# A two-layer decoder trunk: fp32 diagonal blocks in the attention, three kept experts with a tile-pair tail, and a branch prefetch hint

## The chip, the cores and the metric

The kernel runs on one core of a Trainium2 chip. The metric is the device time of one execution in microseconds (us), the median of several runs; lower is better. The engines are TensorE (PE; its weight loads are shown as PEld), VectorE (DVE), ScalarE (ACT), GpSimd (POOL) and SyncE (SP).

## The reference

Two layers work on x, 512 tokens of width 1024 in float32. Each layer is a token mixer and then a mixture of experts, each followed by `x = layer_norm(alpha * x + f(x))`. The mixer of layer 0 is a chunked gated linear attention. That of layer 1 is a sparse attention with three branches (compressed, selected and window), each a causal softmax of the scores times values, mixed by gates. What the change touches, cut down:

```python
smask = (kpos <= qpos[:, None])                       # causal: the diagonal block is half masked
p_slc = masked_softmax(jnp.einsum('bghqd,bgqkd->bghqk', qb, k_sel), smask)
o_slc = jnp.einsum('bghqk,bgqkd->bghqd', p_slc, v_sel)
p_win = masked_softmax(jnp.einsum('bghqd,bgkd->bghqk', qb, kw_b), wmask)
o_win = jnp.einsum('bghqk,bgkd->bghqd', p_win, vw_b)
...
gate = jnp.zeros((n, 16)).at[arange(n)[:, None], top_e].set(w)     # two experts of 16 per token
h = silu(einsum('nd,edf->nef', xt, w_gate)) * einsum('nd,edf->nef', xt, w_up)
return einsum('nef,efd->nd', h * gate[:, :, None], w_down)         # D 1024, hidden 256
...
y = (x - mean) * rsqrt(var + 1e-5) * g + b                         # layer_norm over 1024
```

## The kernel before, in words

The 512 tokens are four tiles of 128 rows, t = 0 to 3. Nearly all products are made of three float16 products: both operands are split into a high and a low float16 part (hi and lo), and hi·hi, hi·lo and lo·hi are summed in a PSUM bank of 512 float32 columns. The splits of the weights (L179 on ACT, L181 on DVE) run beside the products on PE. In time the program is: the linear attention (0 to about 235 us), the experts of layer 0 (to about 412), the projections of the sparse attention and the attention itself (to about 768), the experts of layer 1 (to about 960) and the tail, the last normalisation and the stores.

**The experts** (`moe`). Each expert has 96 slots. For expert e a one-hot matrix of tokens by slots is made on POOL (L828, one instruction per tile), and PE collects the expert's rows with it (L839, 64 matmuls). Gate and up products are L910 to L912, the gate of each slot is summed on PE at L915, the down product is L944 to L946. Experts 0 to 13 write their weighted output to the DRAM buffer `yslots` (ACT copies at L953, a DMA issued by ACT at L955). When expert 13 has been issued, eight indirect DMAs on POOL's queue (L959) gather the rows of `yslots` and add them into x. The last `KEEP = 2` experts, 14 and 15, stay in SBUF as hi and lo (`yh`, L949 on ACT, L950 on DVE). Their one-hot matrices are transposed (L856, L857) to `ohT`, and `add_last` brings their outputs back to the tokens with one-hot products (L359, per tile and half 2 experts x 2 parts) and adds the bank to x: on DVE (L369), or by a copy on ACT (L366) and an add on POOL (L367).

**The fallback** (`dense_moe`). Behind expert 0's gate and up products stands a block for the case that an expert has more than 96 tokens. Every engine loads a number (L966) and compares it (L967); here the block is jumped over in both layers. It holds some 870 of PE's 23,700 instructions.

**The tail** (`finish_out`). All four tiles go through `add_last` (three halves on DVE, five on ACT and POOL). Then, for the pair (0, 1) and then (2, 3), come the statistics of the rows on DVE (L331, L311), the chain of small instructions that ends with the inverse deviation z (L312 to L317, one chain per tile), and the scaling: four halves by two DVE instructions (L344, L345), four by one on ACT (L347) and two on POOL (L348, L349). Each half is then stored (L1574, issued by SP).

**The attention** (`nsa_attn`). It goes over query tiles t = 3, 2, 1, 0, four groups g of four heads, and two branches b. `scores` computes for every key block j up to t the scores (L1418, L1419), the exponential to float32 `pf` (L1421 on ACT), on the diagonal block j = t a mask on POOL (L1424), and the split into `ph` hi and lo: hi on ACT (L1386, a second exponential from PSUM, or L1388, a copy) or DVE (L1390), lo on POOL (L1392) or DVE (L1394), by the turns in `HI_BY` and `LO_BY`. `pv` multiplies each block with V, three matmuls per head and block (L1435 to L1437). `combine` divides and adds (L1458 to L1468, DVE and POOL). `evac_v` writes V from PSUM (L1224 ACT, L1225 DVE). In between PE works on the output projection (L257 to L259).

The order on each engine is that of a scheduler that records the operations. Pools of buffers decide how early a step can start: `ph` lies in the three buffers of the weights' staging tag `wst`.

Of the kernel before, what the change touches and what calls it, by code (L numbers as in the profile page):

```python
# [21 lines left out]
NT = 4  # L22
# [9 lines left out]
PUMPS = (5, 5, 5, 5, 5, 5, 5, 5, 5, 5, 5, 5, 5, 8, 5, 4, 5, 5, 5, 5)  # L32
HI_BY = 'daeeee'
LO_BY = 'pdp'
OUT_ADD = (0, 0), (1, 0), (1, 1), (1, 1)
OUT_DVE = 1, 5, 6, 7
OUT_DIR = -1
# [15 lines left out]
NSU = 4  # L53
NHL = dict(l=4, a=3)
RINGS = "aaallll" * 3 + "aaalllll" * 3 + "aaa", "aaallll" * 7
KEEP = 2
HS = 16.0
NEG = -1e30


class Trunk:
# [258 lines left out]
    def finish_out(self, store):  # L320
        nc = self.nc
        V = nc.vector
        lng, lnb = self.moe_ln
        scales, after = {}, None
        for t in range(NT):
            self.add_last(t, OUT_ADD[t])
        for pair in ((0, 1), (2, 3)):
            for t in pair:
                for n in range(2):
                    with self.behind(after):  # L330
                        last = V.bn_stats(self.bns[t][:, n], self.x[t][:, n * 512:n * 512 + 512])  # L331
            for t in pair:
                with self.behind(last):
                    self.bn = self.bns[t]
                    _, mean, z, b = self.ln_scale()
                    after = V.scalar_tensor_tensor(b, mean, -1.0, z, op0=OP.mult, op1=OP.mult)
                scales[t] = mean, z, b
            for t in pair[::OUT_DIR]:
                mean, z, b = scales[t]
                for h in range(2):  # L340
                    hs = slice(h * 512, h * 512 + 512)
                    s, g, o = self.x[t][:, hs], lng[:, hs], lnb[:, hs]
                    if 2 * t + h in OUT_DVE:
                        V.scalar_tensor_tensor(s, s, mean, g, op0=OP.subtract, op1=OP.mult)  # L344
                        V.scalar_tensor_tensor(s, s, z, o, op0=OP.mult, op1=OP.add)  # L345
                    else:
                        nc.scalar.activation(s, s, AF.Identity, bias=b, scale=z)  # L347
                        nc.gpsimd.tensor_mul(s, s, g)  # L348
                        nc.gpsimd.tensor_add(s, s, o)  # L349
                    store(t, h)  # L350

    def add_last(self, t, pool=()):
        self.bns[t] = self.tmp([P, 2, 6], F32, "bn", 4)
# [456 lines left out]
    def moe(self, layer, xT, ahead=()):  # L810
# [153 lines left out]
    def dense_moe(self, layer, xT, gm, ci):  # L964
        nc, tc, a = self.nc, self.tc, self.a
        load = nc.values_load(ci[0:1, 0:1], min_val=0, max_val=2 * S)  # L966
        with tc.If(load > CAP, preferred_fallthrough_block=False):  # L967
            dm = self.tmp([P, NT, NE], F32, "rt_dm", 1)
            nc.vector.tensor_scalar(dm, gm, IWS / HS, None, op0=OP.mult)
            with tc.For_i(0, NE, 1) as e:  # L970
                buf = self.row("dw")
                st, hl = buf[:, :512], buf[:, 512:].bitcast(F16).rearrange("p (i n) -> p i n", i=2)

                def load_piece(i, c):
                    src = a["moe"][layer, bass.ds(e, 1), i].rearrange("o p f -> (o p) f")
# [12 lines left out]
                for i in range(2):  # L988
                    b = banks[2 * i:2 * i + 2]
                    for c in range(4):  # L990
                        w = load_piece(i, c)
                        for f in range(2):
                            for t in range(NT):
                                o = b[f][:, t * P:(t + 1) * P]
                                for k in range(2):
                                    s = slice(k * 256 + f * P, k * 256 + f * P + P)
                                    x = [xT[t][u][:, c * 2 + k] for u in range(2)]
                                    product(o, [v[:, s] for v in w], x, c == k == t == 0,
                                            (c, k, t) == (3, 1, NT - 1))
# [73 lines left out]
    def nsa_proj(self, first, PT):  # L1073
# [8 lines left out]
        kA = [PT([P, 4, S], f"kA{b}") for b in range(2)]  # L1082
        kB = [PT([P, 4, S], f"kB{b}") for b in range(2)]
        V = [[PT([P, 4, 129], f"V{b}{t}") for t in range(NT)] for b in range(2)]
        qA = [PT([P, NT, 4, P], f"qA{g}") for g in range(4)]
        qB = [PT([P, NT, S], f"qB{g}") for g in range(4)]
        gate = PT([P, NT, 16, 3], "gate", F32)
# [285 lines left out]
        return (kcA, kcB, vc, kA, kB, V, qA, qB, gate), rest  # L1373

    def nsa_attn(self, T, pool, early, rest, kcA, kcB, vc, kA, kB, V, qA, qB, gate):
# [5 lines left out]
        def split(hi, lo, src, ps=None):  # L1381
            i = cnt[0]
            cnt[0] += 1
            how = HI_BY[i % len(HI_BY)]
# [28 lines left out]
        def scores(t, g, b):  # L1413
            ph = self.wp.tile([P, 4, 2, S], F16, name="ph", tag="wst", bufs=NST)
            for j in range(t, -1, -1):
# [4 lines left out]
                pf = T([P, S], "pf", F32, 3)  # L1420
# [5 lines left out]
                split(ph[:, j, 0], ph[:, j, 1], pf, None if j == t else st)  # L1426
            return ph

        def pv(t, g, b, ph):
            ob = self.bank()  # L1430
            for h in range(4):
                hs = slice(h * P, (h + 1) * P)
                o0 = ob[:, h * 65:(h + 1) * 65]
                for j in range(t + 1):
                    nc.tensor.matmul(o0, ph[:, j, 0, hs], V[b][j][:, g, 0:65], start=(j == 0), stop=False)  # L1435
                    nc.tensor.matmul(o0[:, :64], ph[:, j, 0, hs], V[b][j][:, g, 65:129], start=False, stop=False)
                    nc.tensor.matmul(o0, ph[:, j, 1, hs], V[b][j][:, g, 0:65], start=False, stop=(j == t))  # L1437
            return ob

        def cmp_pv(g, pch):  # L1440
# [204 lines left out]
```

## Time and profile before

| what | us |
|---|---|
| runs | 994.8, 988.48, 992.65 |
| median | 992.65 |
| profiled execution, its own time | 996.98 |
| its span | 995.3 |

[...] Over the span PE is busy 87%, DVE 77%, ACT 57%, POOL 36%. In timelines, a row's first number is its start and the second its length in us; in square brackets stands how long the engine was idle before it and what ended that ("issue" is time in which it waited for nothing that the profile shows). A name ending in q, as PEldq, is the sequencer of an engine, which takes branches and issues DMAs.

### The profile page before, as it was taken

What the parts mean: (1) busy time and instruction counts of PE and PEld (TensorE: products, weight loads), DVE (VectorE), ACT (ScalarE), POOL (GpSimd) and SP (SyncE); (2) the same over time, 40 slices, a digit from 0 to 9 for tenths busy, and PEclk for the clock granted to TensorE, in tenths of its full rate; (3) what the DMA queues carried; (4) which work ended last, traced back from release to release, by engine and by line L of the source; (5) the groups of instructions that cost most, each with busy time, mean ns of one, the idle gap of its engine ahead of it and who ended that gap; (6) DMA issues with size and microseconds to landing.
All of it is one profiled execution on the core that took longest, in us unless ns stands there. A gap on an engine that the chain in (4) does not pass through costs nothing. (4 is left out here: it accounts for less than half of the span.)

```text
span 995.3 us, 26759 instructions
## 1 busy us (share of the span) xinstructions
PE 868.1 (87%) x11266; PEld 708.6 (71%) x11266; DVE 767.5 (77%) x1675; ACT 571.5 (57%) x1196; POOL 353.4 (36%) x375
## 2 busy tenths in 40 slices
PE   7999999995799999699989989787987569999960
PEld 2478888875788888488978868465766558988840
DVE  5962226989699998797697756898798969999738
ACT  4832432542499999515535347765447149999821
POOL 0210120023135330540384425686532319523056
PEclk9999999997799999999999999788999679999995
DMA  9652231253499995942330010300018349999282
GB/s 299 222 207 86 85 114 57 86 213 127 142 385 394 368 380 213 213 143 83 128 127 3 2 43 2 129 2 1 2 47 336 128 149 409 380 380 379 100 154 100
DMA packets 29393, 169.64 MB, mean 170 GB/s; under 512 B 3536, under 2 KB 4176, under 8 KB 12752
## 3 DMA queue, kind: packets, MB, share of 16 engines
q1 hardware_dynamic: 23168, 144.49, 38.7%
q0 software_dynamic: 2960, 12.32, 5.7%
q10 hardware_dynamic: 3136, 11.01, 3.0%
q8 instruction: 93, 1.52, 0.6%
q14 instruction: 36, 0.29, 0.1%
HBM read 153.91 MB, written 13.89 MB: 169 GB/s over the span
## 5 line engine op out<-in xcount | busy, mean ns | idle before, releaser
L828 POOL TENSOR_SCALAR ohe<-icap,rt_px 128x96 f16<-128x96 f32 x112 | 111.6, 1011 | 153.2 <-PE bank L915 144.5
L181 DVE SCALAR_TENSOR_TENSOR whl<-wsu,whl 128x512 f16<-128x512 f32 x192 | 127.3, 713 | 3.0 <-ACT whl L179 2.2
L181 DVE SCALAR_TENSOR_TENSOR whl<-wst,whl 128x512 f16<-128x512 f32 x116 | 75.5, 702 | 67.3 <-ACT whl L179 67.2
L839 PE MATMUL bank<-ohe,xs 128*128 128x96 f16 x2048 | 103.7, 215 | 15.6 <-issue 8.6
L839 PEld LDWEIGHTS <-xs 128*128 128x128 f16 x2048 | 98.7, 104 | 16.6 <-issue 12.1
L179 ACT ACTIVATE whl<-wsu 128x512 f16<-128x512 f32 x192 | 106.8, 624 | 3.3 <-PE bank L259 3.2
L179 ACT ACTIVATE whl<-wst 128x512 f16<-128x512 f32 x144 | 80.8, 624 | 29.9 <-PE bank L250 9.8
L181 DVE SCALAR_TENSOR_TENSOR wha<-wst,wha 128x512 f16<-128x512 f32 x144 | 93.9, 703 | 1.7 <-ACT wha L179 1.7
L257 PE MATMUL bank<-whl,xt 128*128 128x256 f16 x320 | 88.1, 275 | 0.8 <-ACT xt L232 0.7
L259 PE MATMUL bank<-whl,xt 128*128 128x256 f16 x320 | 87.4, 274 | 1.4 <-DVE xt L233 1.4
L258 PE MATMUL bank<-whl,xt 128*128 128x256 f16 x320 | 88.1, 275 | 0.0
L179 ACT ACTIVATE wha<-wst 128x512 f16<-128x512 f32 x144 | 79.7, 622 | 2.5 <-DMA wst<-moe 2.5
L910 PE MATMUL bank<-xh,whl 128*128 128x96 f16 x576 | 75.2, 206 | 0.0
L911 PE MATMUL bank<-xh,whl 128*128 128x96 f16 x576 | 75.2, 206 | 0.0
L912 PE MATMUL bank<-xh,whl 128*128 128x96 f16 x576 | 75.2, 206 | 0.0
L259 PE MATMUL bank<-whl,oT 128*128 128x256 f16 x256 | 70.6, 276 | 2.2 <-DVE oT L233 2.2
L257 PE MATMUL bank<-whl,oT 128*128 128x256 f16 x256 | 70.7, 277 | 0.8 <-ACT oT L232 0.5
L258 PE MATMUL bank<-whl,oT 128*128 128x256 f16 x256 | 70.6, 276 | 0.0
L258 PE MATMUL bank<-whl,xT 128*128 128x256 f16 x256 | 69.8, 273 | 0.0
L259 PE MATMUL bank<-whl,xT 128*128 128x256 f16 x256 | 69.8, 273 | 0.0
L257 PE MATMUL bank<-whl,xT 128*128 128x256 f16 x256 | 69.8, 273 | 0.0
L911 PE MATMUL bank<-xh,wha 128*128 128x96 f16 x448 | 62.7, 212 | 4.3 <-issue 4.3
(388 smaller groups left out, 2813.2 us busy)
## 6 DMA issues: line engine op xcount, KB each, us to landing
wsu<-moe SPq DMA_DIRECT2D x54, 1024.0 KB, 7.8
wst<-moe SPq DMA_DIRECT2D x42, 1024.0 KB, 7.9
wst<-gla_in SPq DMA_DIRECT2D x11, 1024.0 KB, 4.8
yslots<-y ACTq DMA_DIRECT2D x28, 384.0 KB, 6.9
wst<-nsa_in SPq DMA_DIRECT2D x9, 1024.0 KB, 4.8
wst<-gla_out SPq DMA_DIRECT2D x4, 1024.0 KB, 4.8
wha<-nsa_out SPq DMA_DIRECT2D x4, 1024.0 KB, 4.9
xs<-xT SPq DMA_DIRECT2D x4, 512.0 KB, 7.1
```

The costliest lines, as they stand in the source:

```text
L179: self.hi_ins = nc.scalar.activation(hl[:, 0, s], st[:, s], AF.Copy, scale=WS)
L181: nc.vector.scalar_tensor_tensor(hl[:, 1, s], st[:, s], WS, hl[:, 0, s], op0=OP.mult, op1=OP.subtract)
L257: nc.tensor.matmul(out, xt[0][:, k], w[0][:, s], start=(k == 0), stop=False)
L258: nc.tensor.matmul(out, xt[0][:, k], w[1][:, s], start=False, stop=False)
L259: nc.tensor.matmul(out, xt[1][:, k], w[0][:, s], start=False, stop=(k == KT - 1))
L828: eng.tensor_scalar(part[e][0][:, t], self.icap, self.px[:, t, e:e + 1], None, op0=OP.is_equal)
L839: nc.tensor.matmul(banks[half][:, j * CAP:(j + 1) * CAP], xs[t][:, i, k * P:(k + 1) * P], oh[:, t], start=(j == 0 and t == self.order[0] a ...
L910: nc.tensor.matmul(o, w[0][:, s], xh[:, 0, k], start=(k == 0), stop=False)
L911: nc.tensor.matmul(o, w[1][:, s], xh[:, 0, k], start=False, stop=False)
L912: nc.tensor.matmul(o, w[0][:, s], xh[:, 1, k], start=False, stop=(k == KT - 1))
```

## The change

Three things are changed.

1. **Attention.** For the diagonal block of t = 0, 1, 2 the exponentials are left in float32, in the 2 x 512 float16 places of `ph` that held hi and lo, and masked there. `pv` multiplies them in one fp32 product per head with a float32 copy of V, `VF`, instead of three float16 ones. `VF` is written by six further ACT copies and six POOL memsets in `evac_v`. The subtraction for lo goes to POOL only for t = 3, otherwise to DVE.
2. **Experts and tail.** `KEEP` is 3: expert 13 stays in SBUF too, and the gathers start behind expert 12. In the tail, tiles 0 and 1 go through `add_last` with all adds on DVE. For tiles 2 and 3 a new `sum_last` also adds x itself on PE, by an fp32 product with the identity matrix, and statistics and scaling read the PSUM bank. The chain for z is computed once for both tiles of a pair, two columns at a time. Three halves, not four, are scaled on ACT and POOL.
3. **Branch.** The fallback's branch carries a label, and a hint for TensorE names it (`mark_branch_hint_location`, once per layer, behind `route`). The option `preferred_fallthrough_block=False` is dropped.

```diff
-KEEP = 2
+KEEP = 3
...
+        for t in (0, 1):
+            self.add_last(t)
+            src[t] = [self.x[t][:, h * 512:h * 512 + 512] for h in range(2)]
+        for t in (2, 3):
+            src[t] = self.sum_last(t)
...
+            for c in (3.0, 12.0, 768.0):
+                V.tensor_mul(u, z, z)
+                V.tensor_mul(u, u, v)
+                V.scalar_tensor_tensor(z, u, c, z, op0=OP.subtract, op1=OP.mult)
...
+                    if (t, h) in OUT_POOL:
+                        nc.scalar.activation(x, s, AF.Identity, bias=b[:, i:i + 1], scale=z[:, i:i + 1])
+                        nc.gpsimd.tensor_mul(x, x, g)
+                        nc.gpsimd.tensor_add(x, x, o)
                     else:
...
+    def sum_last(self, t):
...
+            self.nc.tensor.matmul(ps, self.identf, self.x[t][:, ns], start=True, stop=False)
+            for e in range(KEEP):
+                for i in range(2):
+                    self.nc.tensor.matmul(ps, self.ohT[:CAP, e, t * P:(t + 1) * P], self.yh[e][:CAP, i, ns],
+                                          start=False, stop=(e == KEEP - 1 and i == 1))
...
         gi, gh, gm, ci = self.route()
+        self.tc.mark_branch_hint_location(f"dense{layer}", HINT, [mybir.EngineType.PE])
...
-        with tc.If(load > CAP, preferred_fallthrough_block=False):
+        with tc.If(load > CAP, label=f"dense{layer}"):
...
+                    if tp * 2 + j < NT - 1:
+                        vf = VF[b][tp * 2 + j]
+                        nc.scalar.activation(vf[:, :, 0:64], ps[:, j], AF.Copy, scale=IWS)
+                        nc.gpsimd.memset(vf[:, :, 64:65], 1.0)
...
-            if ps is not None and LO_BY[i % len(LO_BY)] == "p":
+            if share and ps is not None and LO_BY[i % len(LO_BY)] == "p":
...
+                exact = j == t < NT - 1
+                pf = ph[:, j].rearrange("p i q -> p (i q)").bitcast(F32) if exact else T([P, S], "pf", F32, 3)
...
+                if not exact:
+                    split(ph[:, j, 0], ph[:, j, 1], pf, None if j == t else st, t == NT - 1)
...
+                if exact:
+                    pf = ph[:, t].rearrange("p i q -> p (i q)").bitcast(F32)
+                    nc.tensor.matmul(o0, pf[:, hs], VF[b][t][:, g], start=True, stop=(t == 0))
```

How instructions stand on three engines, before and now (line numbers are each kernel's own). First PE at layer 0's fallback in the kernel before; L970 and the rows up to it belong to the fallback's loop, and `wha` and `xh` are expert 0's weights and rows.

```order
L910 LDWEIGHTS wha
L910 MATMUL bank<-xh,wha 128x96
L966 TENSOR_LOAD rt_ci
L967 COMPARE_AND_BRANCH
L967 UNCONDITIONAL_BRANCH
L970 COMPARE_AND_BRANCH
L970 UNCONDITIONAL_BRANCH x2
```

The same place in the changed kernel (L990 is the load, L991 the branch), and the end of the skipped block with what follows it, some 870 rows on.

```order
L934 LDWEIGHTS wha
L934 MATMUL bank<-xh,wha 128x96
L990 TENSOR_LOAD rt_ci
L991 COMPARE_AND_BRANCH
L994 COMPARE_AND_BRANCH
L994 UNCONDITIONAL_BRANCH x2
...
L994 UNCONDITIONAL_BRANCH
L991 UNCONDITIONAL_BRANCH
L1677 BRANCH_PREFETCH_HINT
L935 LDWEIGHTS wha
L935 MATMUL bank<-xh,wha 128x96
```

The compare itself now jumps, where before a jump stood behind it. The hint in the last piece is the one for layer 1: it stands right behind layer 0's skipped block, some 12,840 rows ahead of layer 1's compare. Layer 0's own hint is the second instruction of PE's program, some 3,390 rows ahead of its compare.

Second, ACT's last rows in the kernel before, from expert 13's down product on (`y` goes to DRAM, `yh` is kept, `more` is the copy of a bank for POOL's add, `r_...` are the tiles of x).

```order
L857 COPY ohT<-bank 96x512
L179 ACTIVATE whl<-wsu 128x512
L953 ACTIVATE y<-bank,gslot 96x512 x2
L955 DMA yslots<-y 96x1024
L919 ACTIVATE sg<-bank 128x192
...
L949 ACTIVATE yh<-bank,gslot 96x512 x2
L366 COPY more<-bank 128x512 x5
L347 ACTIVATE r_12610<-r_12610,lnst 128x512
L347 ACTIVATE r_12339<-r_12339,lnst 128x512 x2
L347 ACTIVATE r_11697<-r_11697,lnst 128x512
```

And in the changed kernel (L880, L178, L973 and L353 stand for L857, L179, L949 and L347).

```order
L880 COPY ohT<-bank 96x512
L178 ACTIVATE whl<-wsu 128x512
L973 ACTIVATE yh<-bank,gslot 96x512 x2
L943 ACTIVATE sg<-bank 128x192
...
L973 ACTIVATE yh<-bank,gslot 96x512 x2
L353 ACTIVATE r_12389<-r_12389,lnp 128x512
L353 ACTIVATE r_12145<-r_12145,lnp 128x512
L353 ACTIVATE r_11613<-bank,lnp 128x512
```

Expert 13's DMA is gone, so the last DMA that the gathers wait for is expert 12's; the copies `more` are gone, and the last scaling on ACT reads a bank.

Third, DVE's last rows before: statistics of tiles 2 and 3 (`bn`), the small steps of two chains in turn, and the scaling of tile 3's halves.

```order
L331 BN_STATS bn<-r_11697 128x6 x2
L331 BN_STATS bn<-r_11043 128x6 x2
L311 BN_AGGR lnst<-bn 128x2 x2
...
L344 SCALAR_TENSOR_TENSOR r_11043<-r_11043,lnst,lng 128x512
L316 TENSOR_SCALAR lnst<-lnst 128x1
...
L336 SCALAR_TENSOR_TENSOR lnst<-lnst 128x1
L345 SCALAR_TENSOR_TENSOR r_11043<-r_11043,lnst,lnb 128x512 x2
```

Now:

```order
L358 SCALAR_TENSOR_TENSOR r_12145<-r_12145,lnp,lnb 128x512
L335 BN_STATS bn<-bank 128x6 x3
L337 BN_AGGR lnp<-bn 128x2
L357 SCALAR_TENSOR_TENSOR r_11613<-bank,lnp,lng 128x512
L335 BN_STATS bn<-bank 128x6
L337 BN_AGGR lnp<-bn 128x2
L339 TENSOR_SCALAR lnp<-lnp 128x2
...
L346 SCALAR_TENSOR_TENSOR lnp<-lnp 128x2
L358 SCALAR_TENSOR_TENSOR r_11613<-r_11613,lnp,lnb 128x512
L358 SCALAR_TENSOR_TENSOR r_11036<-r_11036,lnp,lnb 128x512 x2
```

The statistics read banks, and a first scaling step of tile 2 (L357) stands ahead of the last statistics.

## Rows read from the trace of the kernel before

**Rows 1.** The page: the span.

```profile
span 995.3 us, 26759 instructions
```

**Rows 2.** Windows: busy us and instructions of each engine per stretch, granted clock, DMA.

```profile
core 0: us, PE busy (x) PEld busy (x) DVE busy (x) ACT busy (x) POOL busy (x), PEclk, DMA share, GB/s
256.00:264.00 8.00, 6.50 (x85) 6.29 (x83) 2.15 (x5) 2.95 (x9) 2.92 (x4) 0.51 0.38 135
640.00:760.00 120.00, 100.19 (x1250) 75.20 (x1250) 105.37 (x263) 66.67 (x124) 63.52 (x64) 0.89 0.15 58
804.00:813.00 9.00, 5.58 (x65) 5.27 (x66) 2.03 (x4) 1.98 (x7) 0.00 (x0) 0.50 0.26 108
960.00:996.00 36.00, 4.38 (x21) 1.76 (x18) 24.41 (x63) 5.98 (x9) 20.76 (x15) 0.60 0.45 114
```

**Rows 3.** The fallback's branch, L967: PE's sequencer, ns min/median/max, and DVE's.

```profile
L967 PEldq COMPARE_BRANCH  x4: 81/2054/5040, 251.2 to 799.2; - x4
L967 DVEq COMPARE_BRANCH  x4: 47/53/61, 251.2 to 799.1; - x4
```

**Rows 4.** Timeline behind the two branches, PE, and POOL at layer 1.

```profile
255.74 0.26 PE L911 MATMUL bank<-xh,wha 128*128 128x96 f16 x1 [4.26 <-issue]
...
804.29 1.46 PE L839 MATMUL bank<-ohe,xs 128*128 128x96 f16 x16 [5.29 <-issue]
808.88 4.02 PE L839 MATMUL bank<-ohe,xs 128*128 128x96 f16 x48 [3.13 <-issue]
...
799.10 3.54 POOL L828 TENSOR_SCALAR ohe<-icap,rt_px 128x96 f16<-128x96 f32 x4 [7.72 <-PEq L967]
```

**Rows 5.** Timeline of the tail: ACT's last DMAs to DRAM, and POOL.

```profile
931.81 0.31 ACTq L955 DMA_DIRECT2D yslots<-y  x1
941.59 0.31 ACTq L955 DMA_DIRECT2D yslots<-y  x1
...
945.36 1.73 POOL L959 DMA_INDIRECT r<-yslots,rt_gi  x1 [26.28 <-DMA yslots<-y]
...
973.38 2.48 POOL L367 TENSOR_TENSOR r<-r,more 128x512 f32<-128x512 f32 x2 [1.10 <-DMA r<-yslots,rt_gi]
...
990.74 1.59 POOL L349 TENSOR_TENSOR r<-r,lnb 128x512 f32<-128x512 f32 x1
```

**Rows 6.** Timeline of the tail: PE's one-hot products, and DVE.

```profile
957.30 7.07 PE L359 MATMUL bank<-yh,ohT 96*128 96x512 f16 x32
...
958.22 0.75 DVE L950 SCALAR_TENSOR_TENSOR yh<-bank,gslot,yh 96x512 f16<-96x512 f32 x1 [0.50 <-ACT yh L949]
...
969.87 1.29 DVE L331 BATCH_NORM_STATS2 bn<-r 128x6 f32<-128x512 f32 x2 [4.84 <-POOL r L367]
...
987.42 0.28 DVE L317 SCALAR_TENSOR_TENSOR lnst<-lnst 128x1 f32<-128x1 f32 x2
...
988.79 2.41 DVE L345 SCALAR_TENSOR_TENSOR r<-r,lnst,lnb 128x512 f32<-128x512 f32 x2
```

**Rows 7.** Timeline, PE: float32 products of layer 0, 512 and 128 columns.

```profile
22.34 3.60 PE L492 MATMUL bank<-glow,wgu 128*128 128x512 f32 x8
...
41.31 1.05 PE L544 MATMUL bank<-qd,kd 128*128 128x128 f32 x8
```

**Rows 8.** Timeline, PE: two turns of the attention's float16 product with V.

```profile
596.42 0.19 PE L1435 MATMUL bank<-V,ph 128*128 128x65 f16 x1
...
596.52 0.19 PE L1435 MATMUL bank<-V,ph 128*128 128x65 f16 x1
```

**Rows 9.** Groups of 560 to 770 us (busy, mean ns), and L1394's spread.

```profile
L1392 POOL TENSOR_TENSOR ph<-pf,ph 128x512 f16<-128x512 f32 x38 | 51.0, 1348 | 16.4 <-ACT ph L1386 10.2 <-DVE ph L1390 4.2 <-DVE cb L1151 1.3
L1394 DVE TENSOR_TENSOR ph<-pf,ph 128x512 f16<-128x512 f32 x42 | 37.4, 901 | 10.3 <-ACT ph L1388 9.1 <-ACT ph L1386 1.0
...
L1394 DVE TENSOR_TENSOR ph<-pf,ph x42: 662/693/1641, 587.6 to 744.5; 128x512 f16<-128x512 f32 x42
```

**Rows 10.** Timeline between the layers: DVE behind the gathers.

```profile
415.81 1.29 DVE L369 TENSOR_TENSOR r<-r,bank 128x512 f32<-128x512 f32 x2 [3.18 <-DMA r<-yslots,rt_gi]
```

More of the change, by code (lines that the diff above doesn't have):

```diff
@@ L34 @@
 LO_BY = 'pdp'
-OUT_ADD = (0, 0), (1, 0), (1, 1), (1, 1)
-OUT_DVE = 1, 5, 6, 7
-OUT_DIR = -1
+OUT_POOL = (0, 1), (1, 1), (2, 1)
 PRELUDE = ("r0 r1 o0 t2 r2 oa s2 ob rt rs c0 t3 s3 r3 c1 xb",
@@ L55 @@
 RINGS = "aaallll" * 3 + "aaalllll" * 3 + "aaa", "aaallll" * 7
-KEEP = 2
+KEEP = 3
 HS = 16.0
+HINT = mybir.BranchHintType.__args__[0]
 NEG = -1e30
@@ L323, in finish_out @@
         lng, lnb = self.moe_ln
-        scales, after = {}, None
-        for t in range(NT):
-            self.add_last(t, OUT_ADD[t])
+        src = {}
+        for t in (0, 1):
[3 more added lines that the diff above has]
+            src[t] = self.sum_last(t)
+        after = None
         for pair in ((0, 1), (2, 3)):
-            for t in pair:
-                for n in range(2):
+            st = self.tmp([P, 6, 2], F32, "lnp", 2)
+            for i, t in enumerate(pair):
+                for h in range(2):
@@ L330, in finish_out @@
                     with self.behind(after):
[L331 to L345, printed above, removed]
-                    else:
-                        nc.scalar.activation(s, s, AF.Identity, bias=b, scale=z)
-                        nc.gpsimd.tensor_mul(s, s, g)
-                        nc.gpsimd.tensor_add(s, s, o)
+                        V.bn_stats(self.bns[t][:, h], src[t][h])
@@ new lines, in finish_out @@
+                with self.behind(after):
+                    V.bn_aggr(st[:, 0:2, i], self.bns[t].rearrange("p a b -> p (a b)"))
+            mean, var, v, u, z, b = (st[:, i] for i in range(6))
+            V.tensor_scalar(v, var, 2.0 ** 26, EPS / (ALPHA * ALPHA) * 2.0 ** 26, op0=OP.mult, op1=OP.add)
+            V.tensor_scalar(u.bitcast(I32), v.bitcast(I32), 1, None, op0=OP.logical_shift_right)
+            V.tensor_scalar(z.bitcast(I32), u.bitcast(I32), -1.0, float(0x5F3759DF) - 2.0 ** 31, op0=OP.mult, op1=OP.add)
@@ new lines, in finish_out @@
+            for c in (3.0, 12.0, 768.0):
+                V.tensor_mul(u, z, z)
+                V.tensor_mul(u, u, v)
+                V.scalar_tensor_tensor(z, u, c, z, op0=OP.subtract, op1=OP.mult)
+            after = V.scalar_tensor_tensor(b, mean, -1.0, z, op0=OP.mult, op1=OP.mult)
+            for h in range(2):
+                hs = slice(h * 512, h * 512 + 512)
+                g, o = lng[:, hs], lnb[:, hs]
+                for i, t in enumerate(pair):
+                    s, x = src[t][h], self.x[t][:, hs]
+                    if (t, h) in OUT_POOL:
+                        nc.scalar.activation(x, s, AF.Identity, bias=b[:, i:i + 1], scale=z[:, i:i + 1])
+                        nc.gpsimd.tensor_mul(x, x, g)
+                        nc.gpsimd.tensor_add(x, x, o)
+                    else:
+                        V.scalar_tensor_tensor(x, s, mean[:, i:i + 1], g, op0=OP.subtract, op1=OP.mult)
+                        V.scalar_tensor_tensor(x, x, z[:, i:i + 1], o, op0=OP.mult, op1=OP.add)
@@ L350, in finish_out @@
                     store(t, h)
+    def sum_last(self, t):
+        self.bns[t] = self.tmp([P, 2, 6], F32, "bn", 4)
+        out = []
+        for n in range(2):
+            ns = slice(n * 512, n * 512 + 512)
+            ps = self.bank()
+            self.nc.tensor.matmul(ps, self.identf, self.x[t][:, ns], start=True, stop=False)
[3 more added lines that the diff above has]
+                                          start=False, stop=(e == KEEP - 1 and i == 1))
+            out.append(ps)
+        return out
@@ L1084, in nsa_proj @@
         V = [[PT([P, 4, 129], f"V{b}{t}") for t in range(NT)] for b in range(2)]
+        VF = [[PT([P, 4, 65], f"VF{b}{t}", F32) for t in range(NT - 1)] for b in range(2)]
         qA = [PT([P, NT, 4, P], f"qA{g}") for g in range(4)]
@@ L1372, in nsa_proj, with nsa_attn @@
         rest = lambda: v1(0), lambda: v1(1), lambda: cv(0), lambda: cv(1)
-        return (kcA, kcB, vc, kA, kB, V, qA, qB, gate), rest
-    def nsa_attn(self, T, pool, early, rest, kcA, kcB, vc, kA, kB, V, qA, qB, gate):
+        return (kcA, kcB, vc, kA, kB, V, VF, qA, qB, gate), rest
+    def nsa_attn(self, T, pool, early, rest, kcA, kcB, vc, kA, kB, V, VF, qA, qB, gate):
         nc = self.nc
@@ L1379, in nsa_attn, with split @@
         qb = lambda g, t: qB[g][:70, t]
-        def split(hi, lo, src, ps=None):
+        def split(hi, lo, src, ps=None, share=False):
             i = cnt[0]
@@ L1419, in scores @@
                 nc.tensor.matmul(st, kB[b][:70, g, js], qb(g, t), start=False, stop=True)
-                pf = T([P, S], "pf", F32, 3)
+                exact = j == t < NT - 1
+                pf = ph[:, j].rearrange("p i q -> p (i q)").bitcast(F32) if exact else T([P, S], "pf", F32, 3)
                 self.exp_ins = nc.scalar.activation(pf, st, AF.Exp)
@@ L1425, in scores @@
                                             base=0, channel_multiplier=-1)
-                split(ph[:, j, 0], ph[:, j, 1], pf, None if j == t else st)
+                if not exact:
+                    split(ph[:, j, 0], ph[:, j, 1], pf, None if j == t else st, t == NT - 1)
             return ph
@@ L1433, in pv @@
                 o0 = ob[:, h * 65:(h + 1) * 65]
-                for j in range(t + 1):
-                    nc.tensor.matmul(o0, ph[:, j, 0, hs], V[b][j][:, g, 0:65], start=(j == 0), stop=False)
+                exact = t < NT - 1
+                if exact:
+                    pf = ph[:, t].rearrange("p i q -> p (i q)").bitcast(F32)
+                    nc.tensor.matmul(o0, pf[:, hs], VF[b][t][:, g], start=True, stop=(t == 0))
+                last = t if exact else t + 1
+                for j in range(last):
+                    nc.tensor.matmul(o0, ph[:, j, 0, hs], V[b][j][:, g, 0:65], start=(j == 0 and not exact), stop=False)
                     nc.tensor.matmul(o0[:, :64], ph[:, j, 0, hs], V[b][j][:, g, 65:129], start=False, stop=False)
-                    nc.tensor.matmul(o0, ph[:, j, 1, hs], V[b][j][:, g, 0:65], start=False, stop=(j == t))
+                    nc.tensor.matmul(o0, ph[:, j, 1, hs], V[b][j][:, g, 0:65], start=False, stop=(j == last - 1))
             return ob
```

## The prediction

> **What bounds the kernel now.** I read the page's span first, then the windows stage by stage, since the three edits lie in different stages, then the timeline around each edit. The span is 995.3 us [rows 1]; the execution's own time of 996.98 has 1.68 more around it, and the median shown, 992.65, lies 4.33 below it. I do the sum against 996.98 and take 4.33 off at the end.
>
> The windows show three kinds of stage [rows 2]. In the attention (640 to 760) no engine is full: PE is busy 100.2 of 120 us at a mean clock of 0.89, DVE 105.4, POOL 63.5. Who is late changes from step to step there. Behind each of the two fallback branches PE runs at half clock (0.51 and 0.50). In the tail (960 to 996) PE works 4.4 of 36 us, DVE 24.4 and POOL 20.8: that stage is a chain, and work put on PE there costs only where it is late.
>
> The chain of the tail in order of time: ACT issues expert 12's DMA at 931.81 and expert 13's at 941.59; POOL, idle for 26.28 us on that last write, starts the eight gathers at 945.36; POOL adds the last halves at 973.38, released by the last gather; its last scaling ends at 992.33, 2.97 before the span's end [rows 5]. Beside it PE's 32 one-hot products end at 964.37, and DVE waits 4.84 us for POOL's adds before the statistics at 969.87 [rows 6]. The tail is late because of gathers and of adds on POOL, not of products.
>
> **Tail: 12 us less.** *Gathers.* With expert 13 kept they start behind expert 12's DMA, which is 941.59 - 931.81 = 9.78 earlier [rows 5]. From 945.36 to the last landing at about 973.4 they take 28 us; at the same pace they end at 963.6. *PE.* One one-hot product takes 7.07 / 32 = 0.22, and expert 15's last part is ready at 958.22 + 0.75 = 958.97 [rows 6]. Of the 24 products of tiles 0 and 1 six run before that, and 18 x 0.22 = 4.0 leads to 962.9. A float32 product shows two records; L492, four products of 512 columns, has eight records in 3.60, 0.45 each [rows 7]. So a half of tile 2 or 3 takes 2 x 0.45 + 6 x 0.22 = 2.2 and four take 8.8: the last bank is full at 971.7, and the gathers are no longer last. *DVE.* Its four adds (0.65 each), statistics and scalings of pair 0 have from 959 to 971 and lie beside PE. Before, DVE took from 969.87 to 991.20 for two pairs, 10.7 each [rows 6]. For pair 1 now three of four statistics are done beforehand (3 x 0.65 = 1.9 less), one chain of 12 small steps of 0.14 goes (1.7 less), one half more is on DVE but its first step is taken early (about 0.8 more): 7.9, so DVE ends at 979.6. Tile 2's other half goes over ACT and POOL; its factor comes three scalings before DVE's end, about 977, and two POOL steps of up to 1.6 [rows 5] and ACT's one put its end near 981. With the 2.97 behind it the span ends near 983.5, 11.8 less, taken as 12. Bounds: 14 if POOL's half is done before DVE's last; 8 if reading banks in place of SBUF costs DVE half as much again on its eight large reads (2.6) and the gathers keep a little of their old end.
>
> **Branch: 8.5 us less.** PE's compare takes 4 us and more where DVE's takes at most 61 ns [rows 3]; PE then stands idle 4.26 at layer 0 and 5.29 at layer 1, with another 3.13 after sixteen products at layer 1 [rows 4]. Both gaps end with "issue": PE waits for its own instructions. If the hint brings the jump's target in beforehand, layer 0's 4.26 goes, and nothing else is late there: take 4.0. At layer 1 PE cannot gain all 5.29: the next products need POOL's four one-hots, which end at 799.10 + 3.54 = 802.64 [rows 4]. So the first gap gives 804.29 - 802.64 = 1.65. The second gap shrinks without any hint: counted in PE's rows, 48 products instead of 16 now stand between the target and the end of its 256-row piece, and 48 at half clock (1.46 / 16 = 0.09 each) fill the 4.6 us from 804.29 to 808.88. Only 16 are left then, 1.5 us instead of 4.0: 2.6 gained. With the hint the piece's end is reached later still and 1.65 + 2.9 = 4.5 go. Sum 8.5, with PE at half clock behind layer 1's branch as now. If PE also kept full clock there and behind layer 0's, the 64 products would cost some 2.7 instead of 5.8 (3 less) and layer 0's stretch about 2 less: 13.5. If the hint does nothing: 2.6.
>
> The hint of layer 1 stands 12,840 rows ahead of its branch. [...] No row of the kernel before has a hint, so the trace doesn't decide.
>
> **Between the layers: 1.5 us less.** DVE waits 3.18 for the gathers before tile 0's sums at 415.81 [rows 10]. The gathers come earlier as in the tail; PE's sums are 48 instead of 32, and then decide. I take about half of the wait; bounds 0 and 3.
>
> **Experts: 0.3 us more.** Four transposes per layer on PE, a few hundred ns; expert 13's output now takes two ACT and two DVE instructions as 14's does, where the DMA falls away.
>
> **Attention: 3 us less, between 12 less and 12 more.** Removed: 22 subtractions on POOL, at 1.35 each 30 us of its 51; four casts and two subtractions on DVE (some 3.5), and twenty ACT instructions, against six ACT copies and six memsets more. DVE gains in another way: its L1394 has a median of 0.69 and a mean of 0.90 [rows 9], and where POOL reads less, DVE's instructions should come nearer to the median: 42 x 0.2 x 22/38 = 5. Added on PE: 96 float32 products of 65 columns for 288 float16 ones. A float16 triple takes 596.52 - 596.42 = 0.10 [rows 8]; a float32 product of 128 columns takes two records of 1.05 / 8 = 0.13, 0.26 at most with the last one's end, 0.22 by their spacing of 0.11 [rows 7]. If time falls with the columns it is 0.11, otherwise 0.22: 96 times that, less 96 x 0.10, is +1 to +12 us of PE. PE has 20 idle us in 640 to 760, so a part is hidden. DVE's 8.5 less and PE's about 6 more, with neither bounding throughout, make 3 less. The ends: all of PE's 12 more on the end, or DVE's 8.5 and POOL's waits both gone.
>
> [...]
>
> **Sum.** 12 + 8.5 + 1.5 - 0.3 + 3 = 24.7 less: 996.98 - 24.7 = 972.3 by the profile's execution; 4.33 off for the median: 968.
>
> **Rivals.**
> 1. *The hint has no effect.* For it: its place far ahead. Against: the compare itself now jumps. The branch gives 2.6 instead of 8.5: 974. Chance 0.2.
> 2. *The hint hides the fetch and keeps the clock.* 13.5 instead of 8.5, and DVE's splits behind layer 1's branch, idle until PE's sums, follow: 963. Against: POOL's one-hots leave PE idle until 802.64 all the same. Chance 0.12.
> 3. *The attention loses.* Float32 at 0.22 with PE on the end everywhere: 12 more instead of 3 less, 983. For it: PE is busy 100 of 120 us there [rows 2]; against: DVE is busier. Chance 0.12.
> 4. *The tail moves to another wait.* If gathers beside the last experts' products go slower, or reading banks is dear, it gives 5: 975. Against: PE's products end it, not the gathers, by 8 us. Chance 0.08.
> 5. *Slower.* The attention's idle gaps on PE, made longer or more frequent where fp32 blocks wait for POOL's mask, let the granted clock fall to half for most of it. PE's 100 us at 0.89 are 89 at full clock. They fit into 120 us now; to eat the 22 us of the other edits, PE would need 142 us, a mean clock of 89 / 142 = 0.63 instead of 0.89, and for 1% slower 0.58. Only then is it slower: 1003 at 0.58. Against: fewer instructions stand between exponential and product. Chance 0.03.
>
> **How the numbers follow.** The forecast has 0.45. The range reaches from beyond rival 2 with the attention's and tail's better ends, 952, to rival 3, 983; two cases together, as rivals 1 and 3 at 989, lie outside. A measurement of this kernel tells about 1% from no change, here 983 to 1003 around 992.65. Faster by over 1% are all cases but rival 5 and the worst half of 3 and its sums: 0.91; within 1%: 0.06; slower: 0.03.
>
> **What would show it.** Right: the first gather starts some 23 us ahead of the end of expert 15's last split, not 13.6, DVE's last statistics wait for PE and not for POOL, the tail is 12 us shorter counted from expert 15's last split; PE's gap at the branches is under 1 us at layer 0 and ends with POOL's one-hots at layer 1. Wrong: PE's compare still takes 4 us (rival 1), clock 1.00 behind it (rival 2), L1468's float32 products spaced 0.22 with a longer 560 to 770 stretch (rival 3), or a clock under 0.65 there (rival 5).

## The result, and the profile after

The changed kernel takes 963.07 us (median of 4 runs, 962.36 to 964.41), the kernel before beside it 991.13: a ratio of 0.9716 with a 95% interval from 0.968 to 0.9752, 28 us less. The forecast was 968, in a range from 952 to 983. A second series gave 962.51 against 992.49, 0.9706 (0.9673 to 0.9739). The size of the whole came out within 5 us, but not its parts, as the two profiles show.

The changed kernel's page and two of its windows, columns as in [rows 2] (line numbers in rows are each kernel's own):

```profile
span 961.5 us, 26589 instructions
...
PE 881.4 (92%) x11218; PEld 720.3 (75%) x11218; DVE 746.9 (78%) x1662; ACT 558.1 (58%) x1178; POOL 316.8 (33%) x353
```

```profile
640.00:757.00 117.00, 110.98 (x1221) 91.14 (x1220) 94.00 (x267) 61.65 (x114) 38.87 (x45) 0.98 0.21 82
785.00:788.00 3.00, 2.80 (x64) 2.65 (x63) 2.85 (x7) 3.00 (x7) 3.00 (x3) 1.00 0.59 180
```

PE does more work than before (881 against 868 us) and is idle less. In the attention its granted clock, a share of full speed, is 0.98 where it was 0.89, and behind layer 1's branch 1.00 where it was 0.50 [rows 2].

A ledger by stage tells where the 34 us between the two profiles went. Each boundary is the end of one line's last product on PE, or, where a row says first, its start, so it can be found in both traces. The kernel before was profiled three times in all, the changed one twice:

| stage, from the one before to | before, us | changed, us |
|---|---|---|
| layer 0's last router product (L758) | 244.3, 244.3, 243.7 | 246.2, 245.9 |
| first L946 of layer 0's down products: the branch | 21.0, 18.5, 18.1 | 14.0, 14.0 |
| last collecting product (L839) | 124.5, 124.2, 124.2 | 124.4, 124.4 |
| last down product (L946) | 21.3, 21.4, 21.4 | 25.4, 25.0 |
| first compressed-branch product (L1446) | 221.9, 223.3, 223.5 | 222.5, 222.7 |
| layer 1's last router product: the attention | 157.0, 158.3, 158.3 | 143.6, 143.6 |
| first L946 of layer 1's down products: the branch | 24.0, 23.9, 23.9 | 13.3, 13.3 |
| last down product | 143.5, 143.3, 143.2 | 144.5, 144.5 |
| end: the tail | 37.8, 37.9, 37.5 | 27.6, 27.6 |

So the attention gives some 14, layer 1's branch 10.6, the tail 10.2 and layer 0's branch 4 to 7; the end of layer 0's experts takes 4 back. The three profiled executions of the kernel before (995 to 997) lie above its median of about 992, so the parts sum to more than the 28 us of the medians. In which stage its shorter executions are shorter isn't shown, but it is hardly the attention: four kernels below that keep the old attention were profiled at 984 to 992 us, and that stage takes 157.0 in each of them. The stretch to layer 0's router (243 to 246) and the one to the first compressed-branch product (219 to 225) vary from profile to profile whatever the edit. The runs of the kernel before spread from 987 to 999, those of the changed kernel only from 960.6 to 964.4.

### The profile page after: what moved, and what is told of

Its sections match the earlier page's. It is cut to its first block, busy times and chain, and to the rows that moved or that the text cites. A ratio compares the mean times of both kernels' runs of the same rounds, so it can differ in the third digit from the quotient of the medians.

```text
span 961.5 us, 26589 instructions
## 1 busy us (share of the span) xinstructions
PE 881.4 (92%) x11218; PEld 720.3 (75%) x11218; DVE 746.9 (78%) x1662; ACT 558.1 (58%) x1178; POOL 316.8 (33%) x353
## 5 line engine op out<-in xcount | busy, mean ns | idle before, releaser
L178 ACT ACTIVATE whl<-wsu 128x512 f16<-128x512 f32 x192 | 106.7, 624 | 3.5 <-PE bank L258 3.2
L862 PE MATMUL bank<-ohe,xs 128*128 128x96 f16 x2048 | 98.8, 211 | 6.2 <-DVE ohe L851 5.5
L178 ACT ACTIVATE whl<-wst 128x512 f16<-128x512 f32 x144 | 80.8, 624 | 32.4 <-PE bank L249 9.8
L862 PEld LDWEIGHTS <-xs 128*128 128x128 f16 x2048 | 94.3, 101 | 6.7 <-DVE ohe L851 4.5
L178 ACT ACTIVATE wha<-wst 128x512 f16<-128x512 f32 x144 | 79.8, 622 | 4.1 <-DMA wst<-moe 4.1
L258 PE MATMUL bank<-whl,oT 128*128 128x256 f16 x256 | 69.6, 273 | 1.7 <-DVE oT L232 1.7
L256 PE MATMUL bank<-whl,oT 128*128 128x256 f16 x256 | 69.7, 273 | 0.5 <-ACT oT L231 0.5
L257 PE MATMUL bank<-whl,oT 128*128 128x256 f16 x256 | 69.7, 273 | 0.0
```

The lines of the kernel that those rows point to most:

```text
L178: self.hi_ins = nc.scalar.activation(hl[:, 0, s], st[:, s], AF.Copy, scale=WS)
L256: nc.tensor.matmul(out, xt[0][:, k], w[0][:, s], start=(k == 0), stop=False)
L257: nc.tensor.matmul(out, xt[0][:, k], w[1][:, s], start=False, stop=False)
L258: nc.tensor.matmul(out, xt[1][:, k], w[0][:, s], start=False, stop=(k == KT - 1))
L862: nc.tensor.matmul(banks[half][:, j * CAP:(j + 1) * CAP], xs[t][:, i, k * P:(k + 1) * P], oh[:, t], start=(j == 0 and t == self.order[0] a ...
```

## The experiments

**Branch.** First the two hints and the label alone on the kernel before, then the changed kernel without the hints.

```diff
+        self.tc.mark_branch_hint_location(f"dense{layer}", HINT, [mybir.EngineType.PE])
-        with tc.If(load > CAP, preferred_fallthrough_block=False):
+        with tc.If(load > CAP, label=f"dense{layer}"):
```

> The kernel before with the label and the two hints alone. Theory 1 (the hint brings the jump's target in and PE keeps its full clock, as the two traces read side by side: 10.4 us at layer 1's branch, 7 at layer 0's of which 4 are given back before the layer's end): about 13 us less, 977 to 980. Rival 1 (the forecast's term: fetch hidden, half clock at layer 1, POOL's one-hots last): 8.5 less, 982 to 983. Rival 2 (the hint has no effect, only the rows' places count): within 3 us of before, 988 to 991, PE's compare still 4 us long.

> The changed kernel without the two hints; the compare still jumps by itself. Theory 1: the idle time behind both branches comes back (about 4 us at layer 0, 5 at layer 1, half clock behind both) and the time is 10 to 14 us above the changed kernel, 973 to 977. Rival (it is the jump by the compare, or the place of the target in its 256-row piece, and not the hint): within 2 us of the changed kernel, 962 to 965, the compare under 1 us.

The hints alone: 984.08, ratio 0.9904 (0.9877 to 0.9931), 9.5 less. Without them the changed kernel takes 971.04, 0.9794 (0.9756 to 0.9833), against its 0.9716: the hints are worth some 8. That lies near rival 1's 8.5 in the first run and below theory 1's 10 to 14 in the second. PE's compare in the changed kernel, without the hints, and with the hints alone (ns min/median/max), one fence each:

```profile
L991 PEldq COMPARE_BRANCH  x2: 370/681/992, 253.3 to 784.4; - x2
```

```profile
L990 PEldq COMPARE_BRANCH  x2: 3412/3416/3419, 250.5 to 787.6; - x2
```

```profile
L969 PEldq COMPARE_BRANCH  x2: 456/476/497, 253.2 to 794.0; - x2
```

The compare falls from 3.4 us to under 1 in both layers, with the hint of layer 1 some 530 us ahead. That settles the first rival (no effect): it fell. PE behind layer 1's branch, in the changed kernel, without the hints, and with the hints alone:

```profile
784.92 2.88 PE L862 MATMUL bank<-ohe,xs 128*128 128x96 f16 x64
```

```profile
791.17 4.44 PE L862 MATMUL bank<-ohe,xs 128*128 128x96 f16 x64 [3.12 <-PEq L990]
```

```profile
794.63 0.84 PE L840 MATMUL bank<-ohe,xs 128*128 128x96 f16 x16 [0.17 <-PEq L969]
798.01 3.46 PE L840 MATMUL bank<-ohe,xs 128*128 128x96 f16 x48 [2.53 <-issue]
```

In the changed kernel all 64 products run through, at 2.88 / 64 = 0.045 each, at a granted clock of 1.00 (785 to 788). Without the hints PE stops for 3.12 and then runs at 0.069 each. With the hints on the old rows PE starts at once, but stops 2.53 behind sixteen products, at the same place as in [rows 4]. So two things stood in that stretch: the branch itself, and the place of its target.

What PE waits for in these stops can be read from the trace. The program's instructions come by DMA too, and the page of the kernel before counts them:

```profile
q8 instruction: 93, 1.52, 0.6%
```

These are 93 packets of 1.52 MB / 93 = 16 KB. They land ahead of PE's starts, as the next lines show; taken as PE's, that is some 255 of its 23,700 instructions each, close to the forecast's piece of 256 rows. One of them starts at 801.86 and has landed at 802.81, 1.48 us ahead of PE's start at 804.29; the next has landed at 807.32, 1.56 ahead of PE's second start at 808.88 [rows 4]. Behind the branches of the fourteen profiles PE has 28 such stops of over 1.4 us, and it starts again 1.4 to 1.6 us after such a packet has landed each time. (One further stop of that length ends with expert 0's hidden values from ACT.) With the hints, PE's first product at layer 1 comes ahead of any new packet; on the old rows the next packet, from 795.20 to 796.58, is the one that PE waits for until 798.01. By these rows the packet that holds the target is there already, and only the one behind it is missing. Whether the hint fetched it, when, and what keeps it, isn't shown.

To separate the place of the target from chance, the kernel before was profiled twice more:

> The kernel before once more, for a second profile of it. If the long stop behind layer 1's branch (23.9 us from the router's last product to the first down product, 17 to 18 in the kernels whose rows stand elsewhere) hangs on the rows' places, it is 23 to 24 again; if it was chance in a long execution, 17 to 19. The attention from its first compressed product to the router's last is 157 us again by either.

> The same, for a third profile: 23 to 24 us there if the rows' places decide, 17 to 19 if it was chance.

They took 996.65 and 995.49, and the stretch was 23.9 both times. In all kernels with the old rows ahead of that branch and no hint (the one before three times, and two below) it is 23.8 to 24.0; in five others without a hint, whose rows stand elsewhere, 16.6 to 18.0; with hints 17.1 on the old rows and 13.3 in the changed kernel. In these profiles the place of the rows gives 6 to 7 us at layer 1 and the hint another 4; taken in the other order, the hint gives 6.8 and the place 3.8. The times don't show all of the place's part. Below, the second half of the attention's changes and their whole move the rows: by their stages they should take 8 to 10 and 19 to 20 us less than the kernel before, and their times say 1 us more to 5 less, and 8 to 18 less. Part of that is that the profiles of the kernel before lie 3 to 5 us above its median; whether its shorter executions stop at the branch for less isn't shown.

**Attention.** The attention's changes alone, then each of their two halves: subtractions on DVE without float32 blocks, and float32 blocks with the old turns of POOL.

```diff
-            if ps is not None and LO_BY[i % len(LO_BY)] == "p":
+            if share and ps is not None and LO_BY[i % len(LO_BY)] == "p":
...
-                split(ph[:, j, 0], ph[:, j, 1], pf, None if j == t else st)
+                split(ph[:, j, 0], ph[:, j, 1], pf, None if j == t else st, t == NT - 1)   # the first half
+                if not exact:
+                    split(ph[:, j, 0], ph[:, j, 1], pf, None if j == t else st, True)      # the second half
```

> The kernel before with the attention's changes alone. Theory 1 (the two traces' difference from 584 to 747 us is real): 12 to 13 us less, 978 to 980. Rival 1 (the profiled execution of before was long just there, as it lies 5.9 above its median): 6 to 8 less, 983 to 986. Rival 2 (the forecast): 3 less, 988. Rival 3 (float32 products bind): not below 991.

> The kernel before with the attention's subtractions for t = 0, 1, 2 on DVE instead of POOL, and no float32 blocks: 22 subtractions of about 0.7 us go from POOL (1.35 each) to DVE. Theory 1 (the attention's gain comes from the diagonal block's shorter way to PE; DVE is the busiest engine there, 105 of 120 us): 5 to 15 us slower, 998 to 1008. Rival (it comes from POOL no longer slowing DVE): 3 to 8 us faster, 985 to 990, with DVE's subtraction near its median of 0.69. Beside it: PE's program stands as in the kernel before, so if the long stop behind layer 1's branch (23.9 us from the router's last product to the first down product) hangs on the rows' places, it is 23 to 24 again; if it was chance, 17 to 18.

> The kernel before with the float32 diagonal blocks, the other blocks' subtractions shared with POOL by the old turns. Theory 1 (the shorter way of the diagonal block is the gain): 10 to 16 us less, as with the whole of the attention's part. Rival 1 (POOL's relief is the gain): at most 3 less, 988 to 992. Rival 2 (both are needed): about half, 5 to 8 less.

The whole: 977.43, 0.9866 (0.9818 to 0.9915). The first half: 987.49, 0.9946 (0.9915 to 0.9978). The second: 989.99, 0.9979 (0.9948 to 1.001). Both of my first theories fell: subtractions moved to the busiest engine made the kernel faster (987.49, within the rival's 985 to 990), and the float32 blocks alone changed nothing that can be told (989.99, within rival 1's 988 to 992). Part of these times is not the attention's: the whole and the second half move PE's rows, and the stretch behind layer 1's branch is 16.6 and 18.0 instead of 24.0. In the first half it is 23.8. The ledger's attention stage, free of that, is 145.6 for the whole, 155.0 and 154.4 for the halves, 157.0 to 158.3 before: 2 to 4 for each half, 11 to 13 together. The same 110 us of the trace in the kernel before, the first half, the second and the whole:

```profile
640.00:750.00 110.00, 91.77 (x1178) 68.25 (x1179) 97.44 (x242) 59.36 (x110) 63.52 (x64) 0.88 0.07 25
```

```profile
640.00:750.00 110.00, 95.97 (x1175) 70.61 (x1176) 96.36 (x265) 60.23 (x113) 38.94 (x45) 0.83 0.06 24
```

```profile
640.00:750.00 110.00, 105.59 (x1101) 85.67 (x1100) 78.99 (x221) 47.06 (x89) 50.75 (x57) 0.90 0.06 21
```

```profile
640.00:750.00 110.00, 105.48 (x1156) 86.40 (x1156) 88.06 (x258) 54.77 (x102) 32.57 (x42) 0.98 0.17 67
```

The first half frees POOL (63.5 to 38.9) at no cost on DVE (97.4 to 96.4, with 22 subtractions more). Its row for the split on DVE, from 560 to 770 us:

```profile
L1394 DVE TENSOR_TENSOR ph<-pf,ph 128x512 f16<-128x512 f32 x64 | 48.6, 779 | 11.7 <-ACT ph L1388 10.5 <-ACT ph L1386 1.0
```

A subtraction on DVE takes 0.78 in the mean where it took 0.90 [rows 9]. But PE, still waiting, has a clock of 0.83. This profile is weak evidence, though: at 998.41 it is the longest of that kernel's ten executions, whose median is 987.49, and its clock over the span is 0.93, where the others have 0.94 to 0.95. The second half frees DVE (79.0) and fills PE (105.6), at a clock of 0.90: a pause of 2.62 us at 682 is followed by half clock from 685 to 699 (0.66 in the mean over 680 to 700). Only with both is PE busy 105.5 at 0.98. The other profiles agree over these 110 us: in the seven with the old attention the clock is 0.84 to 0.90, in the five with both halves 0.96 to 1.00. That the clock is what joins the two halves is read from these rows; no run changed the clock alone.

**Tail and kept experts.** Together, then the new tail with two kept experts, and three kept experts with the old tail.

```diff
-KEEP = 2
+KEEP = 3
...
+        for t in (2, 3):
+            src[t] = self.sum_last(t)
```

> The kernel before with three kept experts and the new tail alone. Theory 1 (as the two traces read: from expert 15's last split to the end 26.6 instead of 36.3 us, and about 1 us at the layers' border): 10 to 11 us less, 980 to 981. Rival 1 (the forecast): 12 and 1.5 less, 977.5. Rival 2 (the gathers beside the last experts slow the experts' loop in layer 0 and give part back): 6 to 7 less, 984 to 985.

> The kernel before with the new tail (paired chain, tiles 2 and 3 summed on PE) but two kept experts. Theory 1 (the gathers, which still start behind expert 13's write, then end last at about 973 of the old time base, 14 us behind expert 15's last split, and the pair's chain follows): the stretch from expert 15's last split to the end is 31 to 33 us instead of 36.3 and 26.6, the time 4 to 5 us less than before, 988. Rival (the adds on POOL and the two chains were the cost, not the gathers): 27 to 28 us, 8 to 9 less, 984.

> The kernel before with three kept experts and the old tail. Theory 1 (the gathers end 9.8 us earlier, so POOL's adds no longer wait; the two chains and POOL's adds stay): the stretch from expert 15's last split to the end is 31 to 33 us, and layer 0's border gives 4 to 5 back, so the time is within 3 us of before. Rival (POOL's adds and chains bind regardless): 35 to 36 us, and the time is 3 to 5 above before.

Together 985.74, 0.9921 (0.9881 to 0.9962); the new tail alone 990.98, 0.9972 (0.9941 to 1.0003); three kept experts alone 989.62, 0.9981 (0.9943 to 1.0019). From expert 15's last split to the end: 36.3 before, 32.7 with the new tail, 30.4 with three experts, 26.1 with both. The two are worth 3.6 and 5.9, and nearly add. Both stretches fit theory 1 of their run (31 to 33), the second a little better than it; the time of the two together lies by rival 2 (984 to 985). By the times alone this can't be told, since three kept experts move PE's rows (17.8 behind layer 1's branch) and cost 4 to 7 us at the end of layer 0's experts. That cost, in the changed kernel: ACT and PE ahead of the last two experts' down products.

```profile
389.61 4.78 ACT L178 ACTIVATE whl<-wst 128x512 f16<-128x512 f32 x9
...
402.67 2.19 ACT L178 ACTIVATE whl<-wst 128x512 f16<-128x512 f32 x4 [2.27 <-DMA wst<-nsa_in]
404.76 0.67 ACT L973 ACTIVATE yh<-bank,gslot 96x512 f16<-96x512 f32 x1
...
396.02 0.66 PE L968 MATMUL bank<-whl,hh 128*96 128x512 f16 x1 [2.81 <-ACT hh L231]
...
407.20 0.42 PE L968 MATMUL bank<-wha,hh 128*96 128x512 f16 x1 [2.49 <-ACT hh L231]
```

The 4.1 us are three pieces. Ahead of expert 14's down product PE waits 2.81 instead of 1.71: ACT now has nine splits of weights in a row ahead of that expert's gate, where it had six. Behind this pause PE's granted clock is 0.51 from 396.0 to 399.4, and eight products take 0.43 instead of 0.22 each, 1.7 more. Ahead of expert 15's it waits 2.49 instead of 1.21: the gathers start some 8 us earlier in layer 0 too, and there they meet the load of the next stage's weights (`nsa_in`), which takes 7.4 us from issue to landing instead of 4.8. ACT splits these weights in its fixed order, waits 2.27 for them, and behind that wait stand expert 14's last `yh` and expert 15's hidden values. With the tail alone the wait was 4.17. A version for it: two kept experts in layer 0, three in layer 1, and one DRAM buffer for each layer.

```diff
-KEEP = 3
+KEEPS = 2, 3
-        self.yslots = self.dr.tile([SLOTS, D], F32, name="yslots")
+        self.yslots = [self.dr.tile([SLOTS, D], F32, name=f"yslots{i}") for i in range(2)]
+        self.keep, yslots = KEEPS[layer], self.yslots[layer]
```

> The changed kernel with two kept experts in layer 0 and three in layer 1, and a DRAM buffer of its own for each layer. Theory 1 (in layer 0 the earlier gathers run beside the loads of the next stage's weights, ACT waits for these in its order and expert 15 comes late, 4 to 5 us, of which the earlier sums give back about 1): 3 to 4 us below the changed kernel, 959 to 960; the gaps ahead of the last two down products in layer 0 are 1.7 and 1.2 again, not 2.8 and 2.5. Rival (these gaps are hidden behind the layers' border): within 1 us of the changed kernel.

> The changed kernel beside the one with two kept experts in layer 0, on the same chip, for their difference. Theory 1: 963, 3 to 4 above it. Rival: within 1 of it.

It takes 958.67, 0.9669 (0.9636 to 0.9701), the changed kernel beside it 962.51. All six runs (956.9 to 959.34) lie below all six of the changed kernel (960.6 to 963.48). The stage to the last down product is 21.3 again, with gaps of 1.71 and 1.21 ahead of the last two down products; it beats both kernels. ACT's six splits ahead of expert 14's gate are back too, so this run doesn't part the order of ACT from the meeting of the transfers.

## Why the prediction was right, and where its steps were not

*The tail* was forecast at 12 (11.8 by its sum) and gave 10.2. That the gathers and POOL's adds made it late was right; which engine ends it now was not. The changed kernel's last steps on PE, DVE and POOL:

```profile
946.24 1.46 PE L370 MATMUL bank<-yh,ohT 96*128 96x512 f16 x6
...
934.64 0.75 DVE L974 SCALAR_TENSOR_TENSOR yh<-bank,gslot,yh 96x512 f16<-96x512 f32 x1 [0.50 <-ACT yh L973]
...
953.51 3.08 DVE L358 SCALAR_TENSOR_TENSOR r<-r,lnp,lnb 128x512 f32<-128x512 f32 x3
...
912.28 1.73 POOL L983 DMA_INDIRECT r<-yslots,rt_gi  x1 [16.81 <-DVE whl L180]
...
956.12 1.59 POOL L355 TENSOR_TENSOR r<-r,lnb 128x512 f32<-128x512 f32 x1
```

The window from the end of the last split to DVE's end, columns as in [rows 2]:

```profile
935.39:956.59 21.20, 12.31 (x50) 5.31 (x47) 20.22 (x53) 2.30 (x3) 7.24 (x6) 0.90 0.34 100
```

The first gather starts 935.39 - 912.28 = 23.1 ahead of the end of the last split, as forecast (before: 13.6), and the last bank is full 947.7 - 935.4 = 12.3 behind it, against 12.7 forecast. DVE then takes 8.9, not 7.9, its last three scalings 1.03 each beside POOL's two, and from its end to the span's 4.9 pass instead of 3.9. Together these are the missing 1.6. But the sign "DVE's last statistics wait for PE" did not come: the profile shows no wait of DVE from 934.64 to its end at 956.59, where it is busy 20.2 of 21.2 us, and the last statistics start at 948.47, 0.8 behind the last bank. DVE's work on the first pair, which I had put beside PE's products as free, takes as long as they do, so it is DVE's order of work that ends this tail; that the 12.3 came out so near is in part luck.

*The branch* was forecast at 8.5 and gave 15 to 18 by the profiles; by the times the hints alone are worth 8 to 9.5, where I had 5.9 for them. The likeliest case had the hint take away PE's wait for the target: with it PE's compare takes 0.37 to 0.99 us in the changed kernel, without it 3.41 to 3.42, and layer 0 gave its 4 and more. But the likeliest case kept PE at half clock behind layer 1's branch, and the clock there is 1.00: that was the sign of rival 2, at a chance of 0.12, and its 13.5 is the nearer price. Two sizes in layer 1 were wrong besides. I held PE back until POOL's four one-hots ended, and so took 1.65 for the first gap. In the changed kernel PE starts at 784.92, while POOL's four begin at 784.87 and last 3.68: PE does not wait for them, and the whole gap goes. The profile names POOL's one-hots for five of the 28 stops that end behind a packet, but a name there is only inferred. And for the place of the target I took 2.6 where the runs show 6 to 7: without the hints the second stop of 3.13, which waited for a packet of instructions, goes whole, the first is 3.12 instead of 5.29, and the 64 products take 4.44 instead of 1.46 + 4.02; I had reckoned with a part of the second stop only. For the rival that the hint has no effect spoke its place, 12,840 rows ahead; the compare, under 1 us in layer 1 too, speaks against it.

*Between the layers* I forecast 1.5 less; the stage there (221.9 to 223.5 before, 222.5 and 222.7 now) gives nothing that can be told, and layer 0's last experts 4 more. Two steps failed. "The gathers come earlier as in the tail": in layer 0 another load runs at that time, and I counted no one waiting for it (1.3 us). And "0.3 us more" for the experts: I counted instructions and not their order on ACT, which with a third kept expert brings expert 14's gate late (1.1) and, behind that pause, half clock (1.7).

*The attention* was forecast at 3 and gave some 14 in the profiles, beyond my bound of 12. My price of the float32 product was on the cheap side: one product with the three float16 ones behind it, in the changed kernel:

```profile
669.00 0.41 PE L1468 MATMUL bank<-VF,ph 128*128 128x65 f32 x2
669.25 0.19 PE L1471 MATMUL bank<-V,ph 128*128 128x65 f16 x1
```

669.25 - 669.00 = 0.25, also the median of the 60 such products at full clock (0.17 to 0.27), above my 0.11 to 0.22. By that PE got about 96 x 0.15 = 14 us more work, an estimate, and rival 3 had the price nearly right, with the wrong outcome. (A weight load of this product takes 0.19 in the median, one of the float16 product at L1471 0.10.) What failed is the sum "DVE's 8.5 less and PE's about 6 more": it set engine against engine and left out PE's clock. PE was idle 20.8 us between 632 and 752 before and 5.7 after, so its added work went into its pauses, and its clock rose from 0.88 to 0.98 over 640 to 750. Rival 5 had the clock in it, with the wrong sign.

That 968 came within 5 us is in part luck. Too little were the attention's 11 and the branch's 7 or more; against them stand the 4 us given back in layer 0, the 1.5 between the layers and the 2 too much for the tail. By the profiled executions the sum was still 9 us off, 972.3 against 963.17. The 4.33 taken off for the median hid half of that: the changed kernel's profiled execution lies at its median, so nothing was to be taken off on its side.

## What to carry to other kernels

Where PE shares a stage with other engines and the trace shows its clock low there, a second relief can be worth far more than the first: here the halves gave 2 to 4 us each, at a clock of 0.83 and 0.90, and both together 11 to 13, at 0.98. Price edits together, and look at the granted clock beside the busy time. A transfer that is moved earlier meets whatever runs there, as the gathers here ran beside a load that took 7.4 us instead of 4.8; look for an engine with a fixed order that waits for that other transfer, and read that order again behind every edit. An edit far ahead of a branch moves its target's place among the instructions, and that alone was worth 6 us in the profiles here, so an edit measured alone can carry a gain that isn't its own.

## What the runs showed of the hardware that was not expected

A hint given about 530 us and 12,840 rows ahead of its branch still took the compare from 3.4 us to under 1. On the old rows it covered the start of the target only: PE ran sixteen products and then stopped for 2.53 us, until 1.4 us after the next packet of instructions had landed. The same stretch behind layer 1's branch took 23.8 to 24.0 us in five profiles with one placement and 16.6 to 18.0 in five with others. And 22 subtractions moved from POOL to DVE left DVE's busy time as it was, 96.4 against 97.4 us from 640 to 750. From 560 to 770 DVE's subtractions took 0.78 each instead of 0.90, 48.6 in all against 37.4, and beside them L1459 fell from 15.7 to 10.3 and L181 on `whl<-wha` from 16.8 to 13.5.
